# Where the tiles lie in SBUF: weights on multiples of 64 bytes, moving activations beside them

## The chip, the cores and the metric

The kernel runs on one core of a Trainium2 chip. The metric is the device time of one execution in microseconds, as the median of several runs. The engines are named as the profile names them: PE is TensorE's matmul and PEld its weight load, DVE is VectorE, ACT is ScalarE, POOL is GpSimd, SP is SyncE, whose queue issues the weights' DMAs. L180 is line 180 of the kernel before.

## What is computed

Two layers of a decoder trunk over 256 rows of 1024 float32 values. Each layer is a SwiGLU FFN (width 2816), a mixer and a second FFN, with an RMSNorm ahead of and behind each. Cut to what matters:

```python
f = swiglu(rmsnorm(h, g[0]), w_ffn_gu[l, 0], w_ffn_down[l, 0]); h = h + 0.5 * rmsnorm(f, g[1])
z = rmsnorm(h, g[2]) @ w_in[l]            # qk, v, o, i, f, u, sv, xq and the gates
y_m = mlstm(z); y_s = spatial_gating(z); y_x = memory_cross_attention(z, rmsnorm(mem, g[6]))
merged = sum(gates[b] * (y_b @ w_branch[l, b]) for the three branches)
h = h + rmsnorm(merged @ w_out[l], g[3])
f = swiglu(rmsnorm(h, g[4]), w_ffn_gu[l, 1], w_ffn_down[l, 1]); h = h + 0.5 * rmsnorm(f, g[5])
```

## The kernel before

Each float32 operand of a large matmul is kept as two float32r tiles, a high part and a low part, and each product is three matmuls: high by high, high by low, low by high. The weights come in tiles of 512 KB (1024 values, 4096 bytes, in each of 128 partitions): `load_split` issues the DMA into `raw` on SP's queue, ScalarE casts to `hi` (L112), VectorE subtracts to `lo` (L113). There are 4 buffers of `raw` and 6 each of `hi` and `lo`.

There are two forms of product. In `pair_T` (with `cols_T` and `product`, L180) a 128x128 piece of the weights is the stationary operand and 256 columns of an activation (`x[:, kt, :]`, 1024 bytes) move past it; one call is 2 x 8 x 3 = 48 matmuls and needs two weight tiles. In `rows_mm` (L198 to L200) a 128x128 piece of an activation is stationary and 512 columns of the weights move; `full_rows` and `group_rows` are the loops round it.

An FFN calls `pair_T` 22 times on `xh`/`xl`, and `full_rows` on `hh`/`hl` (44 tiles of each kind, in the `tmp` pool) for its down projection. A mixer calls `pair_T` 28 times on `xh`/`xl` (four each for xq, qk, the output gate and u, twelve for the branch gates), `group_rows` on `xh`/`xl` for v and sv, `pair_T` four times on each of `yxh`/`yxl`, `ymh`/`yml` and `ysh`/`ysl` in `branch`, and `full_rows` on `mth`/`mtl`. The memory's keys and values come from `mh`/`ml` by four `pair_T` and two times four `group_rows` in each layer, placed between the stages. The order on TensorE is that of the program. A stage is named by layer and place: `split_x(l, n, pts)` makes `xh`/`xl` for FFN (0,0) with (l, n) = (0, 0), for mixer 0 with (0, 2), for FFN (0,1) with (0, 4), and (1, 0), (1, 2), (1, 4) in layer 1.

In SBUF the tiles of a pool stand one behind another, pool after pool in the order `const`, `stream`, `act`, `tmp`, `small`. A tile's place starts on a multiple of 32 bytes. Up to `mhalf` all sizes are multiples of 64; `mhalf`, 4 bytes, takes 32, so what follows lies 32 bytes past a multiple of 64, until `vm` (8224 bytes, the largest with its tag) brings the rest back:

| tiles before | start, bytes past a multiple of 64 |
|---|---|
| `raw`, `hi`, `lo` | 32 |
| `xh`, `xl`; `mh` and `ysh` (tag `qk`); `ml` and `ysl` (tag `vm`) | 32 |
| `kT`, `ymh`, `vx`, `yml`, `yxh`, `yxl`; `mth`, `mtl` (tags `yxh`, `yxl`) | 0 |
| the buffers of tag `t2`, with `hh` and `hl` | 0 |

Inside a tile every operand of the large matmuls starts on a multiple of 512 bytes.

Of the kernel before, what the change touches and what calls it, by code (L numbers as in the profile page):

```python
# [8 lines left out]
F32 = mybir.dt.float32  # L9
F32R = mybir.dt.float32r  # L10
# [4 lines left out]
P = 128  # L15
D = 1024
KT = D // P
S = 256
# [14 lines left out]
FREE = 4  # L33
BARE_TAIL = 3
BARE_FREE = 3
C_QK, C_V, C_O, C_I, C_F, C_U, C_SV, C_XQ, C_G = 0, 1024, 2048, 3072, 3076, 3080, 4104, 5128, 6152


@with_exitstack
def decoder_trunk(ctx: ExitStack, tc: tile.TileContext, x, mem, norm_g, w_ffn_gu, w_ffn_down, w_in, conv_w,  # L40
# [4 lines left out]
    const = ctx.enter_context(tc.tile_pool(name="const", bufs=1))  # L45
    stream = ctx.enter_context(tc.tile_pool(name="stream", bufs=4))
    act = ctx.enter_context(tc.tile_pool(name="act", bufs=1))
    tmp = ctx.enter_context(tc.tile_pool(name="tmp", bufs=2))
    small = ctx.enter_context(tc.tile_pool(name="small", bufs=4))
# [26 lines left out]
    nc.gpsimd.tensor_copy(sel, sel_f)  # L76
    ones = const.tile([P, P], F32, name="ones")
    nc.gpsimd.memset(ones, 1.0)
    mhalf = const.tile([P, 1], F32, name="mhalf")
    nc.gpsimd.memset(mhalf, -0.5)  # L80
    junk = const.tile([P, 512], mybir.dt.bfloat16, name="junk")
    colA = const.tile([P, 112], F32, name="colA")
# [7 lines left out]
    def g_col(l, n, k):  # L90
        i = (l * 7 + n) * 8 + k
        return colA[:, i:i + 1]
# [7 lines left out]
    def behind(*what):  # L100
        order = ExitStack()
        for ins in what:
            order.enter_context(tc.issue_after(ins.ins))
        return order

    def load_split(src, a, b):
        raw = stream.tile([P, a, b], F32, name="raw", tag="raw", bufs=RAW)
        last["dma"] = nc.sync.dma_start(raw, src)
        hi = stream.tile([P, a, b], F32R, name="hi", tag="hi", bufs=CONV)
        lo = stream.tile([P, a, b], F32R, name="lo", tag="lo", bufs=CONV)  # L110
        with behind(*(hold.pop(0) if hold else [])):
            nc.scalar.copy(hi, raw)  # L112
            nc.vector.tensor_tensor(out=lo, in0=raw, in1=hi.bitcast(F32), op=ALU.subtract)  # L113
        return hi, lo

    def load_cols(w, c0, n):
        his, los = [], []
        for q in range(2):
            hi, lo = load_rows(w, q * 4 * P, 4, c0, n)
            his += [hi[:, k, :] for k in range(4)]  # L120
            los += [lo[:, k, :] for k in range(4)]
        return his, los

    def load_rows(w, r0, k, c0, n):
        return load_split(w[r0:r0 + k * P, c0:c0 + n].rearrange("(k p) c -> p k c", p=P), k, n)
# [33 lines left out]
    def scaled_split(src, gain, hi, lo):  # L159
        last["act"] = nc.scalar.mul(hi, src, gain)  # L160
        last["dve"] = nc.vector.scalar_tensor_tensor(out=lo, in0=src, scalar=gain, in1=hi.bitcast(F32), op0=ALU.mult,  # L161
                                       op1=ALU.subtract)

    def split(src, hi, lo):
        nc.scalar.copy(hi, src)  # L165
        nc.vector.tensor_tensor(out=lo, in0=src, in1=hi.bitcast(F32), op=ALU.subtract)  # L166

    def split_x(l, n, pts):
        xh = act.tile([P, KT, S], F32R, name="xh", tag="xh")
        xl = act.tile([P, KT, S], F32R, name="xl", tag="xl")  # L170
        for kt in range(KT):
            scaled_split(pts[kt // 2][:, kt % 2, :], g_col(l, n, kt), xh[:, kt, :], xl[:, kt, :])
        return xh, xl
# [12 lines left out]
    def pair_T(w, c0, xt):  # L186
        wt = load_cols(w, c0, 2 * P)
        o = ps.tile([P, 2, S], F32, name="o", tag="mm")
        for m in range(2):
            cols_T(o[:, m, :], wt, m * P, xt)  # L190
        return o
# [38 lines left out]
    def boundary(accs, gb, mul, nxt, fill=(), lead=0):  # L230
# [28 lines left out]
        if lead:  # L259
            pts = new_pts()  # L260
            for tt in range(NT):
                transpose_in(xs[tt], tt, pts)
        xt = split_x(*nxt, pts)
        if not lead:
            hold[:] = [[]] * BARE_FREE + [[last["act"], last["dve"]]]
        for f in fill[lead:]:
# [63 lines left out]

    def kv_parts(l):
        def start():
            mh = act.tile([P, KT, S], F32R, name="mh", tag="qk")
            ml = act.tile([P, KT, S], F32R, name="ml", tag="vm")
            for kt in range(KT):
                scaled_split(memT[:, kt, :], g_col(l, 6, kt), mh[:, kt, :], ml[:, kt, :])
            kv[l] = ((mh, ml), [act.tile([P, KT, S], F32R, name="kT", tag=t) for t in ("kT", "ymh")],
                     [act.tile([P, NT, D], F32R, name="vx", tag=t) for t in ("vx", "yml")])

        def k_part(c):  # L340
            mt, kT, vx = kv[l]
            o = pair_T(w_mkv[l], c * 2 * P, mt)
            split(o, kT[0][:, 2 * c:2 * c + 2, :], kT[1][:, 2 * c:2 * c + 2, :])

        os_ = {}

        def v_quarter(c, q):
            mt, kT, vx = kv[l]
            os_[c] = group_rows(w_mkv[l], D + c * 512, mt, (q,), os_.get(c))
            if q == 3:  # L350
                for tt, o in enumerate(os_[c]):
                    split(o, vx[0][:, tt, c * 512:(c + 1) * 512], vx[1][:, tt, c * 512:(c + 1) * 512])

        return start, ([lambda c=c: k_part(c) for c in range(4)] +
                       [lambda c=c, q=q: v_quarter(c, q) for c in range(2) for q in range(4)])

    def mixer(l, xt, nxt, start=None, fill=(), lead=0):
# [20 lines left out]
        wsT = tmp.tile([P, 4, P], F32, name="wsT", tag="wsT", bufs=1)  # L378
        for g in range(4):
            nc.vector.tensor_tensor(out=wsT[:, g, :], in0=wsp[:, g, :], in1=upper, op=ALU.mult)  # L380
        yx = (act.tile([P, KT, S], F32R, name="yxh", tag="yxh"), act.tile([P, KT, S], F32R, name="yxl", tag="yxl"))
        sc = DH ** -0.5

        _, kT, vx = kv[l]
# [37 lines left out]
        vm = act.tile([P, NT, NH, DV + 1], F32, name="vm", tag="vm")  # L422
# [71 lines left out]
        qk = act.tile([P, KT, S], F32, name="qk", tag="qk")  # L494
# [36 lines left out]
                nc.vector.scalar_tensor_tensor(out=mt[1][:, sl, :], in0=mg[:, sl, :], scalar=0.5,  # L531
                                               in1=mt[0][:, sl, :].bitcast(F32), op0=ALU.mult, op1=ALU.subtract)

        ym = (act.tile([P, KT, S], F32R, name="ymh", tag="ymh"), act.tile([P, KT, S], F32R, name="yml", tag="yml"))

        def out_gate(hd):
            so = tmp.tile([P, 2, S], F32, name="so", tag="t2", bufs=T2)
# [26 lines left out]
        def retrieve(hd, sd):  # L564
            nums = [psa.tile([P, 512], F32, name="num", tag="acc") for _ in range(NT)]
            yr = [tmp.tile([P, DV], F32, name="yr", tag="cv", bufs=3) for tt in range(NT)]
            nc.tensor.matmul(nums[0][:, 0:DV + 1], sd[:, 0:P], vm[:, 0, hd, :], start=True, stop=True)
            nc.tensor.matmul(nums[1][:, 0:DV + 1], sd[:, P:S], vm[:, 0, hd, :], start=True, stop=False)
            nc.tensor.matmul(nums[1][:, 0:DV + 1], sd[:, S:S + P], vm[:, 1, hd, :], start=False, stop=True)
            for tt in range(NT):  # L570
                num = nums[tt]
                bst = small.tile([P, 6], F32, name="bst", tag="bst")
                nc.vector.bn_stats(bst, num[:, 0:DV])
                mv = small.tile([P, 2], F32, name="mv", tag="mv")
                nc.vector.bn_aggr(mv, bst)
                dn = small.tile([P, 2], F32, name="dn", tag="dn")
                nc.vector.tensor_scalar(out=dn[:, 0:1], in0=num[:, DV:DV + 1], scalar1=-1.0,
                                        scalar2=emT[:, tt, hd:hd + 1], op0=ALU.mult, op1=ALU.max)
                nc.vector.tensor_tensor(out=dn[:, 1:2], in0=num[:, DV:DV + 1], in1=dn[:, 0:1], op=ALU.max)
                rd = small.tile([P, 1], F32, name="rd", tag="rd")  # L580
                nc.vector.reciprocal(rd, dn[:, 1:2])
                vv = small.tile([P, 1], F32, name="vv", tag="vv")
                nc.vector.scalar_tensor_tensor(out=vv, in0=mv[:, 1:2], scalar=rd, in1=rd, op0=ALU.mult,
                                               op1=ALU.mult)
                nc.vector.tensor_scalar_add(vv, vv, EPS)
                rs = small.tile([P, 1], F32, name="rs", tag="rs")
                nc.gpsimd.tensor_tensor(out=rs, in0=vv, in1=mhalf, op=ALU.pow)  # L587
                nc.vector.tensor_tensor(out=rs, in0=rs, in1=rd, op=ALU.mult)
                nc.vector.tensor_scalar(out=yr[tt], in0=num[:, 0:DV], scalar1=mv[:, 0:1], scalar2=rs,
                                        op0=ALU.subtract, op1=ALU.mult)  # L590
            return yr
# [17 lines left out]
            gated(c, yr, so)  # L609

        vn = act.tile([P, NT, D], F32, name="vn", tag="vx")
        ys = (act.tile([P, KT, S], F32R, name="ysh", tag="qk"), act.tile([P, KT, S], F32R, name="ysl", tag="vm"))
        for c in range(2):
            for tt, o in enumerate(group_rows(w, C_SV + c * 512, xt)):
                nc.scalar.activation(vn[:, tt, c * 512:(c + 1) * 512], o, AF.Gelu_apprx_tanh)
# [41 lines left out]
        for c in range(4):  # L657
            branch(1, 0, ym, c, gate(0, c))
            sgu(c)
        mt = (act.tile([P, KT, S], F32R, name="mth", tag="yxh"), act.tile([P, KT, S], F32R, name="mtl", tag="yxl"))  # L660
        for c in range(4):
            branch(2, 1, ys, c, gate(1, c), mt)
        if start:
# [22 lines left out]
    xt = ffn(0, 1, xt, (1, 0), {}, kv1[3:8], 3)  # L686
    xt = ffn(1, 0, xt, (1, 2), {}, kv1[8:], 3)
    xt = mixer(1, xt, (1, 4))
    ffn(1, 1, xt, None)

# [26 lines left out]
```

## Time and profile before

| | |
|---|---|
| median of 3 runs | 1541.88 us (1540.81 to 1544.29) |
| span of the profiled execution | 1541.1 us |
| instructions | 26328, of them 10870 matmuls with a weight load each |
| busy: PE, PEld | 1521.8 us (99%), 1432.8 us (93%) |
| busy: DVE, ACT, POOL | 929.9 us (60%), 749.1 us (49%), 44.7 us (3%) |
| mean granted clock of TensorE | 0.997 of full speed |
| HBM | 176 GB/s over the span |

The span runs from the first to the last instruction; the time of the execution itself is not recorded beside it, and the median of the other runs is 0.8 us longer. Busy time counts an engine's instructions without counting overlaps twice. TensorE's matmuls are pipelined: the duration of one is longer than the distance to the next one's start, and it is the distances that add up to the span.

### The profile page before, as it was taken

To read this page: it belongs to the slowest core of one execution; us is meant where nothing else is said; L and a number is where in the kernel's file an instruction comes from. 1 tells how busy PE (TensorE), PEld (TensorE's weight loads), DVE (VectorE), ACT (ScalarE), POOL (GpSimd) and SP (SyncE) were. 2 spreads that over 40 slices of the span, in tenths; PEclk is the share of its full clock that TensorE was granted. 3 is DMA by queue.
4 is the path that set the end of the run, shared out by engine and by line. 5 is a ranking of instruction groups with operands and counts; after the bars stand their busy time and mean duration, and the time that the engine had idled before them with its cause. 6 is when DMAs were issued, how large, how long until landed. Compare 5 with 4: busy or idle time off the path is not lost.

```text
span 1541.1 us, 26328 instructions
## 1 busy us (share of the span) xinstructions
PE 1521.8 (99%) x10870; PEld 1432.8 (93%) x10870; DVE 929.9 (60%) x1319; ACT 749.1 (49%) x972; POOL 44.7 (3%) x77
## 2 busy tenths in 40 slices
PE   7999999999999999999999999999999999899998
PEld 7999998999999999999989999898999999799997
DVE  5564575776765567545465554576867665555444
ACT  5544464554444456444464444565544444454442
POOL 1000000000010000000000000000001000000000
PEclk9999999999999999999999999999999999999999
DMA  8656566455566566666656565555555656465652
GB/s 262 208 179 185 182 205 181 135 151 164 152 190 185 170 188 188 181 190 185 187 174 201 183 190 180 184 164 156 149 164 167 187 169 184 129 217 181 189 179 83
DMA packets 222169, 273.49 MB, mean 177 GB/s; under 512 B 12656, under 2 KB 194144, under 8 KB 222048
## 3 DMA queue, kind: packets, MB, share of 16 engines
q1 hardware_dynamic: 221920, 271.75, 58.1%
q8 instruction: 85, 1.39, 0.4%
q14 instruction: 36, 0.29, 0.1%
q10 hardware_dynamic: 128, 0.06, 0.0%
HBM read 270.72 MB, written 1.05 MB: 176 GB/s over the span
## 4 chain that ended last, share of the span: by engine, by line
PE 95%; DVE 2%; DMA 1%; POOL 1%; ACT 1%; issue 0%; SPq 0%; POOLq 0%; DVEq 0%; ACTq 0%
PE o L180 65%; PE acc L198 6%; PE acc L199 6%; PE acc L200 6%; PE o L198 2%; PE o L200 2%; PE o L199 2%; DMA raw<-in_w_ffn_gu_dram 1%; DVE lo L113 1%; PE pts L153 0%; PE mx L641 0%; POOL rs L136 0%; DVE h L244 0%; PE zif L180 0%; POOL rs L587 0%
## 5 line engine op out<-in xcount | busy, mean ns | idle before, releaser
L113 DVE TENSOR_TENSOR lo<-raw,hi 128x1024 fp32r<-128x1024 f32 x504 | 614.0, 1222 | 519.7 <-ACT hi L112 512.5
L112 ACT CAST hi<-raw 128x1024 fp32r<-128x1024 f32 x504 | 527.2, 1050 | 633.4 <-PE o L180 294.0
L180 PE MATMUL o<-xh,hi 128*128 128x256 f32 x2304 | 656.3, 285 | 1.3 <-ACT xh L160 1.1
L180 PE MATMUL o<-xl,hi 128*128 128x256 f32 x2304 | 653.5, 284 | 0.4 <-DVE xl L161 0.3
L180 PE MATMUL o<-xh,lo 128*128 128x256 f32 x2304 | 653.0, 283 | 0.0
L180 PEld LDWEIGHTS o<-xh,hi 128*128 128x128 f32 x2304 | 442.9, 192 | 4.1 <-ACT xh L160 2.0
L180 PEld LDWEIGHTS o<-xl,hi 128*128 128x128 f32 x2304 | 443.0, 192 | 3.2 <-DVE xl L161 1.3
L180 PEld LDWEIGHTS o<-xh,lo 128*128 128x128 f32 x2304 | 443.0, 192 | 0.1
L198 PE MATMUL acc<-hi,hh 128*128 128x512 f32 x352 | 139.4, 396 | 0.0
L199 PE MATMUL acc<-lo,hh 128*128 128x512 f32 x352 | 138.9, 395 | 0.0
L200 PE MATMUL acc<-hi,hl 128*128 128x512 f32 x352 | 138.7, 394 | 0.0
L200 PEld LDWEIGHTS acc<-hi,hl 128*128 128x128 f32 x352 | 66.1, 188 | 16.2 <-DVE hl L166 0.2
L198 PEld LDWEIGHTS acc<-hi,hh 128*128 128x128 f32 x352 | 66.3, 188 | 14.3 <-ACT hh L165 0.3
L199 PEld LDWEIGHTS acc<-lo,hh 128*128 128x128 f32 x352 | 66.1, 188 | 13.9
L198 PE MATMUL o<-hi,xh 128*128 128x512 f32 x128 | 50.2, 392 | 0.0
L200 PE MATMUL o<-hi,xl 128*128 128x512 f32 x128 | 49.9, 390 | 0.0
L199 PE MATMUL o<-lo,xh 128*128 128x512 f32 x128 | 49.8, 389 | 0.0
L136 POOL TENSOR_TENSOR rs<-ms,mhalf 128x1 f32<-128x1 f32 x26 | 16.3, 628 | 1080.5 <-DVE ms L133 1080.5
L165 ACT CAST hh<-hf 128x512 fp32r<-128x512 f32 x44 | 27.3, 620 | 25.5 <-DVE hf L284 25.5
L180 PE MATMUL o<-yxh,hi 128*128 128x256 f32 x128 | 36.6, 286 | 0.0
L180 PE MATMUL o<-mh,hi 128*128 128x256 f32 x128 | 36.4, 284 | 0.0
L180 PE MATMUL o<-ysh,hi 128*128 128x256 f32 x128 | 36.2, 283 | 0.0
(240 smaller groups left out, 1712.8 us busy)
## 6 DMA issues: line engine op xcount, KB each, us to landing
raw<-in_w_ffn_gu_dram SPq DMA_DIRECT2D x176, 512.0 KB, 4.5
raw<-in_w_in_dram SPq DMA_DIRECT2D x144, 512.0 KB, 3.7
raw<-in_w_ffn_down_dram SPq DMA_DIRECT2D x88, 512.0 KB, 4.3
raw<-in_w_branch_dram SPq DMA_DIRECT2D x48, 512.0 KB, 3.6
raw<-in_w_mkv_dram SPq DMA_DIRECT2D x32, 512.0 KB, 4.3
raw<-in_w_out_dram SPq DMA_DIRECT2D x16, 512.0 KB, 4.4
gb<-in_norm_g_dram SPq DMA_DIRECT2D x6, 512.0 KB, 4.7
h<-in_x_dram SPq DMA_DIRECT2D x4, 256.0 KB, 3.1
```

Of the source, the lines that this page charges most:

```text
L112: nc.scalar.copy(hi, raw)
L113: nc.vector.tensor_tensor(out=lo, in0=raw, in1=hi.bitcast(F32), op=ALU.subtract)
L136: nc.gpsimd.tensor_tensor(out=rs, in0=ms, in1=mhalf, op=ALU.pow)
L165: nc.scalar.copy(hi, src)
L180: nc.tensor.matmul(o, u, v, start=(i == 0), stop=(i == n - 1))
L198: nc.tensor.matmul(o, a, u, start=first, stop=False)
L199: nc.tensor.matmul(o, a, v, start=False, stop=False)
L200: nc.tensor.matmul(o, b, u, start=False, stop=last)
```

## The change

`mhalf` gets a slot of 64 bytes, of which the kernel uses the first 4 as before. The activations of `pair_T` get slots 64 bytes longer, and start in them at an offset given in 4-byte words: `placed(name, tag, at)`. For `xh`/`xl` the offset comes from the table `X_AT`, another one for each of the six stages; for `mt` it is 0, for the others 8 words, 32 bytes. `rd` and `vv` become columns of `dn`, which makes room.

```diff
+LINE = 16
+X_AT = {(0, 0): 4, (0, 2): 8, (0, 4): 12, (1, 0): 2, (1, 2): 6, (1, 4): 10}
...
-    mhalf = const.tile([P, 1], F32, name="mhalf")
+    mhalf = const.tile([P, LINE], F32, name="mhalf")[:, 0:1]
...
+    def placed(name, tag, at):
+        t = act.tile([P, KT * S + LINE], F32R, name=name, tag=tag)
+        return t[:, at:at + KT * S].rearrange("p (k s) -> p k s", s=S)
...
-        xh = act.tile([P, KT, S], F32R, name="xh", tag="xh")
-        xl = act.tile([P, KT, S], F32R, name="xl", tag="xl")
+        xh, xl = (placed(name, name, X_AT[l, n]) for name in ("xh", "xl"))
...
-            mh = act.tile([P, KT, S], F32R, name="mh", tag="qk")
-            ml = act.tile([P, KT, S], F32R, name="ml", tag="vm")
+            mh, ml = placed("mh", "qk", 8), placed("ml", "vm", 8)
...
-        yx = (act.tile([P, KT, S], F32R, name="yxh", tag="yxh"), act.tile([P, KT, S], F32R, name="yxl", tag="yxl"))
+        yx = placed("yxh", "yxh", 8), placed("yxl", "yxl", 8)
...
-        ym = (act.tile([P, KT, S], F32R, name="ymh", tag="ymh"), act.tile([P, KT, S], F32R, name="yml", tag="yml"))
+        ym = placed("ymh", "ymh", 8), placed("yml", "yml", 8)
...
-                dn = small.tile([P, 2], F32, name="dn", tag="dn")
+                dn = small.tile([P, 4], F32, name="dn", tag="dn")
...
-                rd = small.tile([P, 1], F32, name="rd", tag="rd")
+                rd = dn[:, 2:3]
...
-                vv = small.tile([P, 1], F32, name="vv", tag="vv")
+                vv = dn[:, 3:4]
...
-        ys = (act.tile([P, KT, S], F32R, name="ysh", tag="qk"), act.tile([P, KT, S], F32R, name="ysl", tag="vm"))
+        ys = placed("ysh", "qk", 8), placed("ysl", "vm", 8)
...
-        mt = (act.tile([P, KT, S], F32R, name="mth", tag="yxh"), act.tile([P, KT, S], F32R, name="mtl", tag="yxl"))
+        mt = placed("mth", "yxh", 0), placed("mtl", "yxl", 0)
```

By these sizes the weights, all slots of the `act` pool and the `t2` buffers start on multiples of 64. The distance of an operand from the weights, modulo 64 bytes:

| operand | before | after |
|---|---|---|
| `xh`, `xl` in FFN (0,0), mixer 0, FFN (0,1) | 0 | 16, 32, 48 |
| `xh`, `xl` in FFN (1,0), mixer 1, FFN (1,1) | 0 | 8, 24, 40 |
| `mh`, `ml`, `ysh`, `ysl` | 0 | 32 |
| `yxh`, `yxl`, `ymh`, `yml` | 32 | 32 |
| `hh`, `hl`, `mth`, `mtl` (stationary only) | 32 | 0 |

## Rows read from the trace of the kernel before

**Rows 1.** The page: busy time of each engine, and the weights' DMA queue.

```profile
PE 1521.8 (99%) x10870; PEld 1432.8 (93%) x10870; DVE 929.9 (60%) x1319; ACT 749.1 (49%) x972; POOL 44.7 (3%) x77
...
q1 hardware_dynamic: 221920, 271.75, 58.1%
```

**Rows 2.** The page: the chain that ended last, by engine and line.

```profile
PE 95%; DVE 2%; DMA 1%; POOL 1%; ACT 1%; issue 0%; SPq 0%; POOLq 0%; DVEq 0%; ACTq 0%
PE o L180 65%; PE acc L198 6%; PE acc L199 6%; PE acc L200 6%; PE o L198 2%; PE o L200 2%; PE o L199 2%; DMA raw<-in_w_ffn_gu_dram 1%; DVE lo L113 1%; PE pts L153 0%; PE mx L641 0%; POOL rs L136 0%; DVE h L244 0%; PE zif L180 0%; POOL rs L587 0%
```

**Rows 3.** Waits of TensorE: us in total, times, longest us.

```profile
PE pts L153 <- DVE xs L147: 6.9, 3, 4.2
PE pt L87 <- POOL mhalf L80: 4.2, 1, 4.2
```

**Rows 4.** Windows, first and last of six stages: busy us, clock, DMA, GB/s.

```profile
0.00:238.00 238.00, 229.85 (x1592) 214.64 (x1593) 137.67 (x167) 123.20 (x167) 8.82 (x26) 1.00 0.65 202
...
1372.00:1541.10 169.10, 162.94 (x1119) 150.79 (x1117) 80.68 (x82) 67.42 (x78) 1.10 (x2) 0.99 0.53 162
```

**Rows 5.** The chain in order of time: start, duration, what and count.

```profile
62.19 11.50 PE o L180 x96
...
513.65 46.07 PE o L180 x384
```

**Rows 6.** Timeline of PE within the first `branch` on `yx`: start, duration.

```profile
347.78 0.28 PE L180 MATMUL o<-yxh,hi 128*128 128x256 f32 x1
...
350.47 0.28 PE L180 MATMUL o<-yxh,lo 128*128 128x256 f32 x1
350.58 0.28 PE L180 MATMUL o<-yxh,hi 128*128 128x256 f32 x1
...
351.17 0.27 PE L180 MATMUL o<-yxh,lo 128*128 128x256 f32 x1
```

**Rows 7.** Timeline of PE in the first `branch` on `ym`.

```profile
447.03 0.28 PE L180 MATMUL o<-ymh,hi 128*128 128x256 f32 x1
...
452.57 0.28 PE L180 MATMUL o<-ymh,lo 128*128 128x256 f32 x1
```

**Rows 8.** The chain: the transposes ahead of a stage.

```profile
593.62 1.75 PE pts L153 x16
```

**Rows 9.** The chain in a down projection (`full_rows`, 512 columns).

```profile
57.29 0.23 PE acc L198
...
61.96 0.23 PE acc L200
```

**Rows 10.** The chain in a projection of v (`group_rows`, 512 columns).

```profile
285.00 0.23 PE o L198
...
290.91 0.23 PE o L200
```

**Rows 11.** Weight loads by tile: duration ns min/median/max, first and last start.

```profile
L180 PEld LDWEIGHTS o<-ysh,hi x128: 192/192/192, 519.1 to 1315.2; 128*128 128x128 f32 x128
...
L180 PEld LDWEIGHTS o<-ymh,hi x128: 188/188/192, 446.9 to 1262.5; 128*128 128x128 f32 x128
```

**Rows 12.** Groups by line: busy us, mean ns of one, idle before.

```profile
L113 DVE TENSOR_TENSOR lo<-raw,hi 128x1024 fp32r<-128x1024 f32 x504 | 614.0, 1222 | 519.7 <-ACT hi L112 512.5 <-PE o L180 6.8
L112 ACT CAST hi<-raw 128x1024 fp32r<-128x1024 f32 x504 | 527.2, 1050 | 633.4 <-PE o L180 294.0 <-issue 174.7 <-PE acc L200 110.7
...
L587 POOL TENSOR_TENSOR rs<-vv,mhalf 128x1 f32<-128x1 f32 x16 | 10.6, 661 | 247.9 <-DVE vv L585 229.7 <-DVE vv L583 18.2
```

**Rows 13.** The matmuls into `num`, all heads and layers: ns min/median/max.

```profile
L567 PE MATMUL num<-vm,sd x16: 377/378/378, 351.3 to 1168.3; 128*128 128x257 f32 x16
```

**Rows 14.** The chain at the `num` matmuls of one head.

```profile
392.06 0.43 PE num L567 x2
```

## Prediction, before the change was run

> **What bounds the kernel now.** I read the page's table of engines first [rows 1]: TensorE is busy in 99% of the span and its weight loads in 93%, VectorE in 60%, ScalarE in 49%, and the DMA queue of the weights takes 58.1% of the 16 engines' time. The chain of work that ended last says the same from the other side [rows 2]: 95% of the span is TensorE, 65% is the line of `product` alone (L180), 24% the three lines of `rows_mm` (L198 to L200). The list of waits of TensorE shows that it hardly ever waits for another engine: the largest sum is 6.9 us [rows 3]. [...] So the time is a number of matmuls times the distance between their starts, and any nanosecond taken off that distance on the chain comes off the end, as long as the weights still arrive.
>
> The busy column can't give that distance, because matmuls overlap: one with 256 columns is booked with 285 ns. The distance comes from the chain, whose pieces give a count and a duration, and from the times of starts.
>
> - 256 columns moving, moving tile and weights on the same offset: `xh`/`xl` run 96 in 11.50 us, and 384 (half `xh`, half `ysh`) in 46.07 us [rows 5]. That is 119.8 and 120.0 ns each.
> - 256 columns, tiles 32 bytes apart: from the first to the last of 30 starts with `yxh`/`yxl` 3.39 us pass [rows 6], 29 distances of 116.9 ns; from the first to the last of 48 with `ymh`/`yml` 5.54 us [rows 7], 47 of 117.9 ns. Mean 117.4; I use 2.6 ns as the saving against 120.0.
> - A stream with half the moving columns: 16 transposes, each with its own weight load of 128 columns, take 1.75 us [rows 8], 109 ns each. [...] I take 109 as the floor, so at most 11 of the 120 ns are to be had.
> - 512 columns moving (here the weights move): in `full_rows` 20 distances in 4.67 us, 233.5 ns; in `group_rows` 26 in 5.91 us, 227.3 ns [rows 9, 10].
>
> The lever is thus real in this trace. `branch` runs the same line with the same shapes on `yx`, `ym` and `ys`. The duration of one of their weight loads is 188 ns where the offsets differ and 192 ns at every count where they agree [rows 11], and the distances follow. The difference between these streams that I see in the code is where the tiles lie.
>
> **The change part by part.** The number of instructions and their shapes stay; no DMA, queue or wait moves. Only addresses do, and the sum is one of columns of the same matmul at another distance.
>
> *The 64-byte slot of `mhalf`* moves all behind it by 32 bytes. Together with the padded slots it puts weights and every slot of the activations on multiples of 64.
>
> *Moving activations that come to 32 bytes.* The mixer of layer 0 has 28 calls of `pair_T` on `xh`/`xl`, 48 matmuls each, 1344; `mh`/`ml` have 128 of each of three kinds, 384, and `ysh`/`ysl` as many. These 2112 go from 120.0 to the distance of the `yx`, `ym` rows: 2112 x 2.6 ns = 5.5 us less (2112 x 2.1 = 4.4 to 2112 x 3.1 = 6.5). `yx` and `ym` themselves stay 32 bytes away from the weights, and keep their distance.
>
> *Moving activations at 8, 16, 24, 40 and 48 bytes.* Each FFN has 22 x 48 = 1056 such matmuls: 16 bytes in FFN (0,0), 48 in (0,1), 8 in (1,0), 40 in (1,1); the mixer of layer 1 has 1344 at 24. Together 4 x 1056 + 1344 = 5568, the largest share by far, and no row has these offsets. From below the floor bounds them: 11 ns x 5568 = 61 us less. From above I take the largest effect of a layout that a row shows, 233.5 - 227.3 = 6.2 ns, as a loss: 35 us more. Of the values known, 0 bytes is the one without gain and 32 the only other; the rows for 32 are the nearest in kind (a different offset), so I take 2.6 ns: 5568 x 2.6 = 14.5 us less. If the gain grew evenly with the distance to a multiple of 64, it would be 0.65 ns at 8, 1.3 at 16 and 48, 1.95 at 24 and 40, and the sum 1056 x 5.2 + 1344 x 1.95 = 8.1 us; that is inside the range.
>
> *Stationary activations under 512 moving weights.* The `full_rows` stationaries (`hh`, `hl` of the four FFNs, 1056 matmuls, and `mth`, `mtl`, 192) lay 32 bytes from the weights and come to 0; those of `group_rows` (`xh`/`xl` in both mixers, 384, and `mh`/`ml`, 192) lay on 0 and come to 24 or 32. If the 6.2 ns between [rows 9] and [rows 10] belong to the offset, 1248 x 6.2 = 7.7 us are won and 576 x 6.2 = 3.6 us lost, 4.1 us less. In this trace the offset and the form of the loop go together in every such matmul, so the 6.2 ns may belong to the loop; then this part is 0. I take 4.1, and 0 stays in the range.
>
> *`rd` and `vv` inside `dn`, `mhalf` as a slice.* The same instructions on the same engines. GpSimd reads `vv`, and a slot of `dn` is used again four allocations, two heads, later; GpSimd is busy in 3% of the span [rows 1]. Cost nothing; were its cover gone it would be one VectorE write behind one GpSimd power, 0.66 us [rows 12], in 16 places 10.6 us at the very worst.
>
> *Feeding a faster TensorE.* One stretch of an FFN (two `pair_T`, two `down`) takes 11.50 us for 96 matmuls and 5.6 for 24 [rows 5, 9], 17.1 us, for six weight tiles. VectorE needs 6 x 1222 ns = 7.3 us for them and ScalarE 6 x 1050 = 6.3 us [rows 12]. A stretch shorter by even the full 11 ns each would be 16.0 us. Nothing new becomes the bound.
>
> Sum: 5.5 + 14.5 + 4.1 = 24.1 us off the profiled span of 1541.1, 1517.0. That execution stands 0.8 us under the median of the runs, 1541.88; so the median forecast is 1517.8, rounded 1518.
>
> **The rivals.**
>
> *The layout does nothing (within 3 us).* The 2 to 3 ns of `yx` and `ym` would then belong to something else, such as higher address bits, and the 6.2 ns to the loop. For it: `yx` and `ym` have the same offset and still differ by 1 ns. Against it: `ymh` and `ysh` lie in the same function and loop. Time 1542. [...]
>
> *An offset off the 16-byte grid costs (slower).* 8, 24 and 40 bytes, FFN (1,0), mixer 1 and FFN (1,1): 2 x 1056 + 1344 = 3456 matmuls. If they lose the 6.2 ns, 21.4 us are paid, against 5.5 + 4.1 + 2112 x 2.6 = 15.1 us won elsewhere: 1541.9 + 6.3 = 1548. It decides from 15.1 / 3456 = 4.4 ns a matmul on. Against it: the `num` matmuls read `vm` at starts 0, 4, 8 and 12 bytes past such a multiple (rows of 257), and all 16 last 377 to 378 ns [rows 13]. But those stream at half the speed, 0.22 us for 257 columns [rows 14], so it isn't excluded. [...]
>
> *Near the floor.* If some of the new offsets take the weight load's reads wholly out of the moving stream's way, the stages of layer 1 and perhaps more come to about 110: 5568 x 8 ns = 44.5 us, with 5.5 and 4.1 besides 54 us: 1488. For it: single distances among the `yx` starts are 0.11 us [rows 6]; against it: no stream of full width averages under 116.9.
>
> **How the numbers follow.** Chances: the gain of the sum, between 1495 and 1538.8, 0.68; near the floor, below 1495, 0.13; no difference, 0.10; slower by the grid, 0.09. About 0.2%, 3.1 us, is what a measurement of this kernel can tell from no change. So faster 0.81, same 0.10, slower 0.09. The likeliest case gives 1518; its own range is 1500 to 1533. The range that leaves out 0.1 on either side is 1493 to 1541.
>
> **What would show it right or wrong.** The pieces of the chain, one stage after the other: 96 matmuls of an FFN in 11.25 us in place of 11.50 (117.4 ns), and four FFNs with four different numbers if the offset sets them; `mh` and `ys` at 117 to 118 ns with weight loads of 188; `full_rows` at 227 and `group_rows` at 233. Wrong would be: the FFNs at 120 (no effect), over 122 in layer 1 alone (the grid), under 112 (the floor), or new waits of TensorE for the weights' tiles.

## The result

The changed kernel takes 1532.33 us (4 runs, 1531.97 to 1532.8) where the kernel before took 1542.09 beside it: ratio 0.9939, 95% interval 0.9925 to 0.9953. It is faster, by 9.8 us or 0.6%, clear of the spread of the runs; 24 were forecast.

### The profile page after: what moved, and what is told of

Read it like the earlier page. It is cut to its first block, busy times and chain, and to the rows that moved or that the text cites. A ratio compares the mean times of both kernels' runs of the same rounds, so it can differ in the third digit from the quotient of the medians.

```text
span 1530.3 us, 26328 instructions
## 1 busy us (share of the span) xinstructions
PE 1511.3 (99%) x10870; PEld 1425.0 (93%) x10870; DVE 930.2 (61%) x1319; ACT 749.6 (49%) x972; POOL 44.7 (3%) x77
## 3 DMA queue, kind: packets, MB, share of 16 engines
q1 hardware_dynamic: 221920, 271.75, 59.2%
## 4 chain that ended last, share of the span: by engine, by line
PE 96%; DVE 1%; POOL 1%; DMA 0%; ACT 0%; issue 0%; SPq 0%; POOLq 0%; DVEq 0%; ACTq 0%
PE o L185 66%; PE acc L205 6%; PE acc L203 6%; PE acc L204 6%; PE o L203 3%; PE o L205 3%; PE o L204 3%; PE pts L159 1%; DMA raw<-in_w_ffn_gu_dram 0%; PE mx L645 0%; DVE lo L115 0%; PE zif L185 0%; POOL rs L142 0%; POOL rs L591 0%; DVE h L249 0%
## 5 line engine op out<-in xcount | busy, mean ns | idle before, releaser
L185 PE MATMUL o<-xh,hi 128*128 128x256 f32 x2304 | 653.1, 284 | 1.2 <-ACT xh L166 1.1
L185 PE MATMUL o<-xl,hi 128*128 128x256 f32 x2304 | 651.0, 283 | 0.2 <-DVE xl L167 0.2
L185 PE MATMUL o<-xh,lo 128*128 128x256 f32 x2304 | 647.8, 281 | 0.0
L185 PEld LDWEIGHTS o<-xh,hi 128*128 128x128 f32 x2304 | 438.0, 190 | 3.8 <-ACT xh L166 1.9
L185 PEld LDWEIGHTS o<-xl,hi 128*128 128x128 f32 x2304 | 436.5, 189 | 2.5 <-DVE xl L167 0.8
L185 PEld LDWEIGHTS o<-xh,lo 128*128 128x128 f32 x2304 | 436.8, 190 | 0.1
L205 PE MATMUL acc<-hi,hl 128*128 128x512 f32 x352 | 137.4, 391 | 0.0
L203 PE MATMUL acc<-hi,hh 128*128 128x512 f32 x352 | 137.1, 390 | 0.0
L205 PEld LDWEIGHTS acc<-hi,hl 128*128 128x128 f32 x352 | 66.0, 188 | 14.2 <-DVE hl L172 0.2
L203 PEld LDWEIGHTS acc<-hi,hh 128*128 128x128 f32 x352 | 66.2, 188 | 12.9 <-ACT hh L171 0.3
L203 PE MATMUL o<-hi,xh 128*128 128x512 f32 x128 | 50.7, 396 | 0.0
L205 PE MATMUL o<-hi,xl 128*128 128x512 f32 x128 | 50.4, 393 | 0.0
L185 PE MATMUL o<-yxh,hi 128*128 128x256 f32 x128 | 36.7, 287 | 0.0
L185 PE MATMUL o<-ml,hi 128*128 128x256 f32 x128 | 36.3, 283 | 0.0
L185 PE MATMUL o<-yxl,hi 128*128 128x256 f32 x128 | 36.2, 283 | 0.0
```

The lines of the kernel that those rows point to most:

```text
L185: nc.tensor.matmul(o, u, v, start=(i == 0), stop=(i == n - 1))
L203: nc.tensor.matmul(o, a, u, start=first, stop=False)
L205: nc.tensor.matmul(o, b, u, start=False, stop=last)
```

## The profile after

The page's table of engines and chain, and the waits of TensorE in us in total, times, longest. `product` is now L185, `rows_mm` L203 to L205.

```profile
span 1530.3 us, 26328 instructions
...
PE 1511.3 (99%) x10870; PEld 1425.0 (93%) x10870; DVE 930.2 (61%) x1319; ACT 749.6 (49%) x972; POOL 44.7 (3%) x77
...
PE 96%; DVE 1%; POOL 1%; DMA 0%; ACT 0%; issue 0%; SPq 0%; POOLq 0%; DVEq 0%; ACTq 0%
PE o L185 66%; PE acc L205 6%; PE acc L203 6%; PE acc L204 6%; PE o L203 3%; PE o L205 3%; PE o L204 3%; PE pts L159 1%; DMA raw<-in_w_ffn_gu_dram 0%; PE mx L645 0%; DVE lo L115 0%; PE zif L185 0%; POOL rs L142 0%; POOL rs L591 0%; DVE h L249 0%
...
PE pts L159 <- DVE xs L153: 6.5, 2, 4.2
```

The picture of [rows 1 to 3] stays: TensorE from end to end, no new wait. So the 10.8 us between the spans lie in the distances of starts. The chain in order of time (start, duration, what and count), with one stretch of each FFN, one `branch` on `yx`, the gates with `ysh` in layer 0, and the two 512-column forms:

```profile
60.20 11.40 PE o L185 x96
...
281.19 0.23 PE o L203
...
287.93 0.23 PE o L205
...
341.62 5.89 PE o L185 x48
...
509.19 45.36 PE o L185 x384
...
640.64 11.32 PE o L185 x96
...
651.96 0.23 PE acc L203
...
657.21 0.23 PE acc L205
...
844.05 11.35 PE o L185 x96
...
1381.90 11.60 PE o L185 x96
```

Against 11.50 us in [rows 5], the four FFNs take 11.40, 11.32, 11.35 and 11.60 for the same 96 matmuls: 118.8, 117.9, 118.2 and 120.8 ns. The layout counts, the FFNs differ by it, and the last one is slower than before. The `branch` on `yx` takes 5.89, although its offset modulo 64 did not change; in the chain before it took 5.81:

```profile
345.64 5.81 PE o L180 x48
```

`full_rows` came to 228.3 ns (23 distances in 5.25 us) and `group_rows` to 232.4 (29 in 6.74): they have changed places with [rows 9, 10].

From the start times of all matmuls in the two traces I took the mean distance by stage and operand, without distances over 140 ns (260 for 512 columns), where a stream is interrupted. "Offsets" are those of high and low half from the weights, modulo 256 bytes.

| matmuls | offsets before | ns | offsets after | ns | us |
|---|---|---|---|---|---|
| FFN (0,0), 1056 | 0, 0 | 119.85 | 16, 80 | 118.78 | -1.1 |
| mixer 0, 1344 | 0, 0 | 119.82 | 32, 96 | 117.88 | -2.6 |
| FFN (0,1), 1056 | 0, 0 | 119.84 | 48, 112 | 117.93 | -2.0 |
| FFN (1,0), 1056 | 0, 0 | 119.83 | 8, 72 | 118.26 | -1.7 |
| mixer 1, 1344 | 0, 0 | 119.81 | 24, 88 | 119.83 | 0.0 |
| FFN (1,1), 1056 | 0, 0 | 119.84 | 40, 104 | 120.84 | +1.1 |
| `mh`, `ml` 384; `ysh`, `ysl` 384 | 0, 0 | 119.9; 120.0 | 160, 224 | 118.5; 118.5 | -1.1 |
| `yxh`, `yxl`, 384 | 32, 32 | 116.7 | 160, 224 | 118.4 | +0.6 |
| `ymh`, `yml`, 384 | 32, 32 | 117.9 | 32, 96 | 117.9 | 0.0 |
| 512 columns: `hh`, `hl`, 1056 | 32 | 233.0 | 0 | 228.1 | -5.2 |
| 512: `mth`, `mtl`, 192 | 32, 32 | 233.3 | 128, 192 | 233.3 | 0.0 |
| 512: `xh`, `xl` 384; `mh`, `ml` 192 | 0, 0 | 227.1; 227.2 | 32, 96 and 24, 88; 160, 224 | 231.7; 232.5 | +2.8 |
| `vx` against `pT`, 96 | 0, 0 | 119.1 | 192 | 115.0 | -0.4 |

The sum is -9.6 us. The rest, 1.2 us, is the balance of what the means leave out; its largest parts are the long distances, 2.6 us less in FFN (0,0) and 1.1 us more in FFN (1,1). Those of FFN (0,0) lie at the first weights and vary from run to run: its third stretch starts at 45.10 us before and 43.31 after, and between 42.93 and 45.53 in the first six runs below.

The column of offsets holds what the prediction had overlooked: a slot of 8256 bytes is 32 x 256 + 64, so each slot puts its successor 64 bytes farther modulo 256, and the low half 64 bytes farther from the weights than the high one. If 256 and not 64 bytes is the period, `yx` did move, `ys`, `mh` and `yx` share one place (118.4 to 118.5 ns, all three), and `ym` shares that of mixer 0 (117.9, both). That was the theory to test.

## The experiments

Two versions below have four executions each, which spread over 3.0 and 4.8 us; the others have one, so a single time is good to some 2 to 3 us. The distances are good to 0.1 ns, as long as a stretch keeps the same pattern of starts (see below). The kernel before, run beside each, took 1541.6 to 1542.9 us.

**Both halves at the same offset.** `xh` and `xl` become parts of one tile, each stage keeps its offset:

```diff
-        xh, xl = (placed(name, name, X_AT[l, n]) for name in ("xh", "xl"))
+        both = act.tile([P, 2 * KT * S + X_PAD], F32R, name="xx", tag="xx")
+        xh, xl = (both[:, at:at + KT * S].rearrange("p (k s) -> p k s", s=S)
+                  for at in (X_AT[l, n], X_AT[l, n] + KT * S))
```

> The high and the low half of xh/xl stand in one tile, so that both have the same distance from the weights; in the changed kernel the low half stands 64 bytes farther than the high one. The stages keep 16, 32, 48, 8, 24, 40 bytes. Theory A (only the distance modulo 64 bytes counts): the mean distance of starts of the 256-column matmuls stays as in the changed kernel, 118.8, 117.9, 117.9, 118.3, 119.8, 120.8 ns in this order of stages. Theory B (the distance counts over a longer period, at least 256 bytes, and 64 more is another place): the six numbers change by 0.5 ns or more in most stages, mixer 0 at 32 and 32 bytes to the 116.7 to 117.9 of yx and ym in the kernel before. The stationary hh, hl come to 192 bytes modulo 256: A 228 ns, B 233 as mth, mtl at 128 and 192 in the changed kernel.

1534.54 us. At 16, 32, 48, 8, 24, 40 bytes the stages have 118.35, 116.83, 118.34, 119.99, 120.16, 119.21 ns. Mixer 0 fell by 1.0 ns, FFN (1,0) rose by 1.7 and FFN (1,1) fell by 1.6; the other three moved by 0.3 to 0.4, less than the 0.5 that B had forecast for most. Modulo 64 is not enough, since A allows no change. `hh` at 192 came to 229.4 to 233.0 by FFN, between the two forecasts.

**Multiples of 64 bytes.** The same with `X_AT` at 64, 192, 128, 256, 128, 320 bytes.

> As the run before, with distances that are multiples of 64 bytes for both halves: 64, 192, 128 in FFN (0,0), mixer 0, FFN (0,1), and 256, 128, 320 in layer 1. Theory A (modulo 64): all six stages at the 119.8 to 120.0 ns of the kernel before. Theory B (modulo 256): 256 in FFN (1,0) at 120 as distance 0; 320 in FFN (1,1) as 64 in FFN (0,0); 128 the same in FFN (0,1) and mixer 1; 192 in mixer 0 at 114 to 116, because the matmuls of vx and pT, 192 apart in the changed kernel, came from 119.1 to 114.6.

1528.62 us. A stretch of each FFN in the chain, in the order 64, 128, 256, 320:

```profile
62.33 11.31 PE o L188 x96
...
655.19 11.52 PE o L188 x96
...
843.95 11.50 PE o L188 x96
...
1380.56 11.30 PE o L188 x96
```

Modulo 64 all four are the same place. They are not: 64 and 320 give 117.8 ns, 256 gives 119.9 as 0 did, mixer 0 at 192 gives 115.2. So the period is longer than 64 bytes, and these pairs fit 256. The FFNs alone would fit 128 too (0, 128 and 256 at 119.9), but the sweep below excludes it: 112 and 240, both in mixer 1, are 2.9 ns apart, and 96 and 224, both in FFNs, 1.6. The one miss of theory B: 128 gave 119.9 in the FFN and 118.7 in the mixer.

**The place itself, without the distance.** `mhalf` back to 4 bytes; all tiles behind it lie 32 bytes lower.

```diff
-    mhalf = const.tile([P, LINE], F32, name="mhalf")[:, 0:1]
+    mhalf = const.tile([P, 1], F32, name="mhalf")
```

> Undoes one part of the change: mhalf is 4 bytes again, so weights, activations and all behind them lie 32 bytes lower, with the same distances from each other. Theories A and B (distances count): every stage within 0.1 ns of the changed kernel, the span 1530. Rival C (the place itself counts, weights on multiples of 64): the 256-column stages and the 512-column matmuls change by 1 ns or more, up to 8 us in the span.

1530.82 us; the six stages at 118.71, 117.84, 117.93, 118.26, 119.81, 120.82 ns, `hh` at 228. A common shift by 32 bytes changes no distance by more than 0.1 ns. Rival C falls: here weights on multiples of 64 bytes are worth nothing by themselves.

**All offsets 0 in the padded slots.**

```diff
-X_AT = {(0, 0): 4, (0, 2): 8, (0, 4): 12, (1, 0): 2, (1, 2): 6, (1, 4): 10}
+X_AT = {(0, 0): 0, (0, 2): 0, (0, 4): 0, (1, 0): 0, (1, 2): 0, (1, 4): 0}
...
-            mh, ml = placed("mh", "qk", 8), placed("ml", "vm", 8)
+            mh, ml = placed("mh", "qk", 0), placed("ml", "vm", 0)
```

and so for `yx`, `ym`, `ys`.

> Undoes the other part: all offsets in the padded slots are 0, weights and slots stay on multiples of 64. Theory A (modulo 64): all 256-column matmuls at 120 ns, the stationaries hh, hl and those of group_rows at 227 to 228: 1541 less 5 us, 1536. Theory B: xh at 0 and xl at 64 leave 120 ns; ys, mh and yx, all at 128 and 192 modulo 256, share one number, and ym at 0 and 64 has the number of xh, xl.

1528.42 us, 3.9 less than the change. `xh`/`xl` at 0 and 64 run 117.8 to 118.3 in all stages, `ym` (0 and 64 too) 117.8; `ys` 120.8, `yx` 120.2, `mh` 119.9 to 120.7 at 128 and 192. Theory A, 120 ns for all of them, falls; B holds for `ym`, and nearly for the three that should share one number. The step of 64 bytes between the slots, alone, brings `xh`/`xl` 12.5 us by their distances; with the table of offsets, in the change, the two bring 6.3.

**Round 192, and off the grid of 16 bytes.** The one-tile form with other `X_AT`.

> Both halves of xh/xl in one tile at 160, 176, 208 bytes from the weights in layer 0 and 224, 240, 96 in layer 1. Theory B1 (a smooth minimum of the distance over a period of 256 bytes, lowest near 192, where 115.2 ns were measured): 176 and 208 at 115 to 117, 160 and 224 at 116 to 118, 240 at 118 to 119, 96 near 119. Theory B2 (192 is a single place where the two reads fit): all six at 117.5 to 120. Where several stages come under 116, the span comes under 1525.

> The same with 184, 200, 188 in layer 0 and 80, 112, 144 in layer 1: the first two lie 8 bytes off the multiples of 16, the third 12. Theory G (starts off the 16-byte grid cost, as 8, 24 and 40 at 119.2 to 120.2 ns against 16, 32 and 48 at 116.8 to 118.3 in the first run suggest): 184, 200 and 188 at 1.5 ns or more above the 115.2 of 192. Theory B1 without the grid: the three within 0.7 ns of 115.2. 80, 112 and 144 lie between 117.8 (64) and 119.9 (128) by B1.

1532.35 and 1535.36 us. With the runs before, equal halves (M a mixer, F an FFN):

| offset | 0 | 8 | 16 | 24 | 32 | 40 | 48 | 64 | 80 | 96 | 112 |
|---|---|---|---|---|---|---|---|---|---|---|---|
| ns | 119.9 F | 120.0 F | 118.4 F | 120.2 M | 116.8 M | 119.2 F | 118.3 F | 117.8 F | 119.2 F | 119.9 F | 114.3 M |

| offset | 128 | 144 | 160 | 176 | 184 | 188 | 192 | 200 | 208 | 224 | 240 |
|---|---|---|---|---|---|---|---|---|---|---|---|
| ns | 119.9 F, 118.7 M | 118.6 F | 118.4 F | 119.2 M | 119.9 F | 118.6 F | 115.2 M | 120.2 M | 118.0 F | 118.3 F | 117.1 M |

Apart from 0, each offset stood in one stage or two, so the table is a rough order and no more: 192, at 115.2 in mixer 0, has a mean of 116.7 to 117.1 in the FFNs of the version with 192 below.

B1, the smooth minimum, falls: 176 and 208 lie at 119.2 and 118.0, and 112, for which it had 117.8 to 119.9, is the lowest of all. B2, a single good place, falls with 112 as well. G holds in part: with equal halves no offset that is an odd multiple of 8 gains more than 0.7 ns. But multiples of 16 lie anywhere between 114.3 and 119.9, so the grid is no rule for finding a good one.

The starts show why no curve fits. At 192 the stretches of mixer 0 have means of 113.3 or 117.8 ns and nothing between; 115.2 is their mixture. In a stretch the distances repeat, 113, 113, 114 or 118, 118, 117, 118, 118, 117, 119 over and over. Before, `xh` stood at 120, 120, 120. One layout can have more than one such pattern; `yx` and `ym`, both at 32 bytes before, kept two different ones, with means of 116.7 and 117.9.

**Versions from the sweep.** Both halves of `xh`/`xl` at 112, or at 192, in all stages; `mh`, `ys`, `ym`, `yx`, `mt` at 192; `hh` at 0. The first:

```diff
-X_AT = {(0, 0): 4, (0, 2): 8, (0, 4): 12, (1, 0): 2, (1, 2): 6, (1, 4): 10}
+PRE, X_AT, X_PAD, Q_AT = 24, 4, 8, 16
...
+    nc.gpsimd.memset(tmp.tile([P, 16], F32, name="gap", tag="gap", bufs=1), 0.0)
...
-    def placed(name, tag, at):
-        t = act.tile([P, KT * S + LINE], F32R, name=name, tag=tag)
+    if PRE:
+        nc.gpsimd.memset(act.tile([P, PRE], F32, name="pre", tag="pre"), 0.0)
+
+    def placed(name, tag):
+        at, size = {"qk": (Q_AT, KT * S + Q_AT), "vm": (0, KT * S + 64)}.get(tag, (0, KT * S))
+        t = act.tile([P, size], F32R, name=name, tag=tag)
...
-        xh, xl = (placed(name, name, X_AT[l, n]) for name in ("xh", "xl"))
+        both = act.tile([P, 2 * KT * S + X_PAD], F32R, name="xx", tag="xx")
+        xh, xl = (both[:, at:at + KT * S].rearrange("p (k s) -> p k s", s=S) for at in (X_AT, X_AT + KT * S))
```

The calls of `placed` lose their offset. The second has 48, 0, 0, 0 in the first line.

> A version built on the sweeps: both halves of xh/xl 112 bytes modulo 256 from the weights in all six stages, mh/ml, ysh/ysl, ymh/yml, yxh/yxl and mth/mtl at 192, hh/hl at 0. Theory B3 (the distance modulo 256 sets which repeating patterns of starts exist, and what ran just before picks one of them): mixers at 114.3 ns as mixer 1 at 112, ys, mh, yx, ym between 113.3 and 117.8, the FFNs at 114 if their stretches of 96 fall into the same pattern and at 118 if not. hh at 228, mth at 229, the stationaries of group_rows at 230 to 233. Span 1497 with the FFNs at 114, 1514 with the FFNs at 118. If the low place at 112 was a property of mixer 1 and not of the distance, the FFNs stay at 119 to 120 and the span over 1520.

> The same with both halves of xh/xl at 192 in all six stages. Theory B3: the mixers at 115.2 ns in the mean, with stretches at 113.3 and at 117.8 as mixer 0 showed at 192; the FFNs, never tried at 192, all at one of the two; span 1500 with the FFNs at 113.3, 1518 with them at 117.8. In both cases no stretch of 48 or more matmuls has a mean between 114 and 117.

With 112: 1493.16 us, ratio to the kernel before 0.9687 (0.967 to 0.9703). With 192: 1505.94 us, 0.9765 (0.9751 to 0.978). The profiled span with 112, 1489.0 us, lies 8 us under the 1497 that B3 had for FFNs at 114; `ys`, `ym` and `yx` came to 113.5 to 113.7, near the lower end of their range. The chain with 112, an FFN stretch in layer 0, the gates with `ys`, and an FFN stretch in layer 1:

```profile
span 1489.0 us, 26330 instructions
...
74.70 10.92 PE o L191 x96
...
497.15 43.83 PE o L191 x384
...
1362.44 10.92 PE o L191 x96
```

96 in 10.92 us are 113.7 ns: the same in all four FFNs, 114.4 in both mixers. The low place at 112 belongs to the layout, not to mixer 1. `group_rows` pays 233.2 ns for it. With 192, stretches of FFN (0,1) and (1,0):

```profile
613.91 11.31 PE o L191 x96
...
788.50 21.79 PE o L191 x192
...
815.74 11.31 PE o L191 x96
```

At 788.50 stand the first two stretches of FFN (1,0), at 113.5 ns. The FFNs are thus not all at one of the two numbers, as B3 had it. Of the 36 stretches that follow a `full_rows` in the four FFNs, 35 take 11.31 us, 117.8 ns, with the same tiles; the other one, 11.13, has the transposes of the memory ahead of it, and behind its first long distance its starts run at 113.5 ns too.

**What ran just before.** The version with 192, and an unused transpose between `full_rows` and the next stretch:

```diff
+            if j > 1:
+                kick = ps.tile([P, 512], F32, name="kick", tag="mm")
+                nc.tensor.transpose(out=kick[:, 0:P], in_=ident, identity=ident)
             pa = pair_T(w, j * 2 * P, xt)
```

> The version with xh/xl at 192 in all stages, with one unused transpose of 128 columns put ahead of the first pair_T of each FFN stretch from the third on (9 in each FFN, 36 in all); no tile moves. In that version the first stretches of an FFN, behind the transposes, run at 113.3 ns and those behind full_rows at 117.8. Theory B3 (what ran just before picks one of two patterns of the same layout): the stretches behind the inserted transpose change to 113.3, 96 in 10.9 us in place of 11.31, and the span falls by 36 x 0.43 = 15 us less some 0.2 us for each transpose, to 1491 to 1498. Rival (the pattern belongs to the place in the FFN, or to what the other engines do at that time): they stay at 117.8 and the span grows by 4 to 8 us, to 1508 to 1512.

1497.82 us. From the chain:

```profile
60.85 11.31 PE o L191 x96
77.72 10.90 PE o L191 x96
...
612.29 10.90 PE o L191 x96
...
628.65 0.11 PE kick L292
628.76 10.90 PE o L191 x96
```

31 of the 36 stretches changed from 11.31 to 10.90 us and one from 11.13 to 11.00: all 18 in FFN (0,1) and (1,0), and 7 of 9 in each of the others. An added matmul of 0.11 us in 36 places makes this kernel faster, 1497.82 us where the version without it took 1502.61 to 1507.4. The pattern is thus not set by the place in the FFN. The extra tile also shifts which of the four buffers of `ps` an output gets; that isn't what decides, because without it each two stretches in turn use all four, and in FFN (1,0) the first two run at 113.5 ns and the next two at 117.8.

The expectation has the first stretches of an FFN behind transposes. Only those of FFN (0,0) and (1,1) stand directly there; ahead of FFN (1,0) are 24 matmuls of 512 columns on `mh`/`ml`, ahead of FFN (0,1) 48 of 256 columns on them. And what ran just before is not all: up to the third stretch of FFN (0,0) the two programs are the same, yet its first two ran at 113.4 ns in the version without the transpose and at 117.8 in the one with it; those of FFN (1,1) did likewise. In just these two FFNs the next two, behind the first two inserted transposes, stayed at 11.31 us. What else picks the pattern is open.

## Why the prediction was wrong

- *What bounds the kernel, and that a nanosecond off the distance comes off the end:* right. The table of distances accounts for 9.6 of the 10.8 us, and no engine or DMA takes over, not even at 1489 us: there TensorE is busy in 99% of the span, VectorE in 62%, and the weights' queue takes 60.1%. The mean granted clock is 0.997 in all three spans.
- *The layout does nothing:* not so; the same instructions run at 113.7 to 120.8 ns by layout alone. That the reads of the two operands get in each other's way, as the floor rival supposes, is not shown: the runs give distances by layout, not what makes them.
- *Offsets 8, 16, 24, 40 and 48 at the price of 32 bytes:* the step that failed. 14.5 us were forecast, 3.7 measured (-1.1, -2.0, -1.7, 0.0, +1.1). I took two points of an unknown function, 0 and 32, for "same" and "different". 32 was one of the better offsets, with equal halves or not; 24 and 40 belong to those with little gain or none. The 64 bytes between the halves, which the prediction missed, are not what failed this step: with equal halves at the same offsets the five stages gain 3.2 us. The bounds, +6.2 and -11 ns, held.
- *2112 matmuls at 32 bytes:* 5.5 forecast, 3.7 measured (2.6, 0.5, 0.6). With both halves at 32, mixer 0 did get 116.8; the change put the low half at 96, and `mh` and `ys` at 160 and 224. That `yx` keeps its distance failed for the same reason, +0.6.
- *512 columns:* that the offset counts, right; the size, 4.1 forecast and 2.4 measured. `hh` gained 4.9 ns each and `group_rows` lost 4.6 (`xh`, `xl`) and 5.3 (`mh`, `ml`), so most of the 6.2 ns belonged to the offset and not to the loop; with both at 0, 228.1 and 227.1, 1.0 ns is left. `mt` gained nothing: at 128 and 192 it isn't on the weights' place, though it is modulo 64.
- *The grid rival, whose 16 bytes were a supposition:* layer 1, with the three offsets off the grid, gained 0.6 us in all and did not lose, and the sweep doesn't show that it is the grid: mixer 1 and FFN (1,1) at 119.8 and 120.8, FFN (1,0) at 118.3, none of them near the 4.4 ns loss that would decide.
- *Near the floor:* not in this change, but it was in reach. One offset for `xh`/`xl` in all stages, with the other activations at 192, brought 113.7 ns in the FFNs and 48 us.
- *The sign of being right, 11.25 us for 96 at 117.4 ns:* 96 x 117.4 is 11.27.

The fault of method: the prediction argued modulo 64 because the change speaks of 64 bytes. [rows 6, 7] already held the warning, two streams at one offset with 116.9 and 117.9 ns; I averaged them. And 32 bytes stood for every offset, though no row had another.

## What to carry to other kernels

Where TensorE streams matmul after matmul, each with its own weights, see whether the distance of the starts depends on where the moving tile lies against the stationary one, as it did here, with 113.7 to 120.8 ns for 256 columns: take it from the start times, stage by stage, and compare streams of one shape with each other. Look for a good offset by a sweep, with operands that differ only in it, and try a good one in every stage before trusting it; check the period and the padding that a slot adds. And read a mean of distances for what it is: here two stretches of one layout ran in two patterns, at 113.5 and 117.8 ns.

## What the runs showed that I had not expected

- Many undisturbed stretches have one of a few means, 113.3, 116.7, 117.8 or 120.0 ns, and keep it to the end while ScalarE, VectorE and the DMA queue of the weights (49%, 61% and 59.2% of the changed kernel's span) come and go beside them; others, as at 160 bytes with 118.4, run through longer sequences. What sets the means is not shown. Moving the tiles against each other changed the means of the stages (113.7 to 120.8 ns); moving all of them together by 32 bytes changed none by more than 0.1 ns.
- The 109 ns of the transposes, with half the moving columns, which the prediction took as the floor [rows 8], were not reached; 113.3 was the lowest in 22 offsets.
- An extra matmul of 0.11 us was worth 0.41 us to the 96 behind it, in 31 of 36 places.
- The same instructions in the same order, on the same layout, ran at 113.4 ns in one execution and at 117.8 in another.
